# Stick-breaking attention: the scan's carry read in place, its copy and the constant column on GpSimd, v's high part on ScalarE

## The chip, the cores and the metric

The kernel runs on one core of one Trainium2 chip. A core has five engines that run side by side, each with its own in-order queue: TensorE (PE in the profile, with its weight loads as PEld), VectorE (DVE), ScalarE (ACT), GpSimd (POOL) and SyncE (SP), which here only issues DMAs. They share the on-chip memory SBUF (128 partitions) and, GpSimd excepted in this kernel, the accumulators' memory PSUM. The metric is the device time of one execution in microseconds (us); lower is better.

## The reference

One transformer block over 2048 tokens of width 1024, in float32. A projection gives two groups of heads. Four heads are differential attention (two softmax maps a head). Eight heads are stick-breaking attention, which is what the change touches:

```
z = q k^T * scale
mask = k_pos < q_pos
log_1mb = where(mask, log_sigmoid(-z), 0)
rem = cumsum from the right(log_1mb) - log_1mb
a = where(mask, exp(log_sigmoid(z) + rem), 0)
y = a @ v
```

So the weight of key s for query t is beta(t, s) = sigmoid(z) times the product of (1 - beta(t, j)) over all keys j between s and t. Then come the output projection, and a SwiGLU feed-forward of width 2816, each added to the residual trunk.

## The kernel before

Numbers are carried as a high and a low float16 part, so each product is three float16 matmuls. The heads are worked in eight groups: 0 to 3 are the differential heads, 4 to 7 hold two stick-breaking heads each. A generator `proj_stream` projects x for the groups tile by tile (128 tokens), and runs ahead of the attention, so that the projection of group g + 1 is interleaved with the attention of group g. Groups 4 to 6 are projected "turned" (`proj_turned`, q and k come out transposed), and every second tile `turned_out` (L345) takes q, k and v out of PSUM: ScalarE and VectorE write q's parts (L349, L350), and `split_psum` (L357) writes the high and low parts of k and of v. The high part goes to ScalarE (L360) or VectorE (L362), whichever `pick` finds to have the smaller sum of noted costs so far; the low part, which subtracts the high one, is always VectorE (L363). `pick` keeps these sums (`load`) for ScalarE, VectorE and GpSimd; `level` sets them to zero at every fourth row tile of the attention.

Stick-breaking attention (`sb_attn`, L595) goes over 16 row tiles i of 128 queries, over blocks b of up to 1024 keys from the right to the left, and over the two heads m. That is 48 blocks a group. One block is `stage_a` (L602):

- Two tiles of 1028 columns are taken, `be` and `om`, from one ring of nine buffers (`z4`, L263) which holds the block's products and its running products.
- Column n of `om`, right of the last key, gets the value with which the running product begins: the constant 8192 (a VectorE memset, L607) in a row's first block, else a copy of column 0 of the same head's block to the right (a VectorE tensor_copy, L609). Row tiles 8 to 15 have two blocks a head, so of a group's 48 blocks 32 set the constant and 16 copy.
- For each chunk of up to 512 keys, from the right: PE computes the scores into one of four PSUM buffers `sc` (L506, and L508 for the mask); ScalarE writes 1 - beta to `om` (L618) and beta to `sc` or to `be` (L619); VectorE runs the product scan from right to left in place in `om`, which begins with the column right of the chunk (L621); and beta times the running product one column to the right goes to `be` (L622).
- The product L622 is on GpSimd when the block has a second chunk and the group is 4 to 6 (`aside`), else on VectorE. It reads column n of `om` in the chunk that ends at n.
- `split_t` (L449) casts `be` to float16 on ScalarE (L89), makes the low part on GpSimd (L98), and has SP issue a transposing DMA to `aT` (L460).

`stage_b` then multiplies `aT` with v on PE (L517), five to seven blocks later. Every fourth row tile (in group 7 every second) `finish` normalizes the result.

The order on each engine is not the order of the program text. The tile framework collects all instructions with their dependences, and a planner lays them out by a simulated time line (`TileContext(nc, schedule_with_timeline_sim=True)`), with priorities given by the `pri` decorators: `stage_a` stands 200 places ahead (`PRI["at"]`). The framework also puts in the semaphore waits between engines and within one, and the waits for the release of a buffer. So each changed instruction is planned anew along with what is around it.

Of the kernel before, what the change touches and what calls it, by code (L numbers as in the profile page):

```python
# [16 lines left out]
ALU = mybir.AluOpType  # L17
# [4 lines left out]
S, D, P = 2048, 1024, 128  # L22
# [37 lines left out]
def block(tc, a, out):  # L60
    nc = tc.nc
    PE, ACT, DVE, POOL, SP = nc.tensor, nc.scalar, nc.vector, nc.gpsimd, nc.sync
    top = ExitStack()
    with top:
# [35 lines left out]
        def pri(k):  # L100
            def deco(f):
                @functools.wraps(f)
                def g(*args):
                    with tc.high_priority(PRI[k]) if PRI[k] else nullcontext():
                        return f(*args)
                return g
            return deco

        def nm(s):
            uid[0] += 1  # L110
            return f"{s}{uid[0]}"

        def c1(n=1, name="c"):
            t = cp.tile([P, n], F32, name=nm(name))
            return t
# [10 lines left out]
        mhalf = c1(16, "mh")  # L126
        DVE.memset(mhalf[:], -0.5)

        half = c1(2, "half")
        DVE.memset(half[:], 0.0)  # L130
        for m in range(2):
            DVE.memset(half[64 * m : 64 * m + 64, m : m + 1], 2.0 ** -11)

# [122 lines left out]
        with ExitStack() as ph1:  # L256
# [6 lines left out]
            def z4():  # L263
                return zp.tile([P, 1028], F32, tag="z4", bufs=ZB, name=nm("z4"))
# [79 lines left out]
            @pri("po")  # L344
            def turned_out(pq, pv, qT, kT, v, j):  # L345
                two = slice(j - 1, j + 1)
                q2, k2 = (pq[:, 256 * c : 256 * c + 256].rearrange("p (t n) -> p t n", t=2) for c in range(2))
                for m in range(2):
                    ACT.mul(qT[:, m, two, :], q2, half[:, m : m + 1])  # L349
                    DVE.scalar_tensor_tensor(qT[:, 2 + m, two, :], q2, half[:, m : m + 1], qT[:, m, two, :], op0=ALU.mult, op1=ALU.subtract)  # L350
                note("A", 800)
                note("D", 800)
                split_psum(kT[:, 0, two, :], kT[:, 1, two, :], k2, 256)
                vv = v[:, two, :].rearrange("p t (h s e) -> p t h s e", h=2, s=2)
                split_psum(vv[:, :, :, 0, :], vv[:, :, :, 1, :], pv[:, :256].rearrange("p (t h e) -> p t h e", t=2, h=2), 256)

            def split_psum(hi, lo, src, n):  # L357
                sc = 2.0 ** -11
                if pick(A=0.84 * n + 60, D=1.05 * n + 70) == "A":
                    ACT.mul(hi, src, sc)  # L360
                else:
                    DVE.tensor_scalar(hi, src, sc, None, op0=ALU.mult)  # L362
                DVE.scalar_tensor_tensor(lo, src, sc, hi, op0=ALU.mult, op1=ALU.subtract)  # L363
                note("D", 1.05 * n + 70)
# [230 lines left out]
            def sb_attn(g, G):  # L595
                last = {}
                front = []
                wide = [0]
                lag = PD + 2 if g < NG - 2 else PD

                @pri("at")
                def stage_a(i, m, b):  # L602
                    L = (i + 1) * 128
                    n = min(1024, L - 1024 * b)
                    be, om = z4(), z4()
                    if b == i // 8:
                        DVE.memset(om[:, n : n + 1], 8192.0)  # L607
                    else:
                        DVE.tensor_copy(om[:, n : n + 1], last[m][:, 0:1])  # L609
                    last[m] = om  # L610
                    for c in range((n - 1) // 512, -1, -1):
                        lo, hi = 512 * c, min(512 * c + 512, n)
                        w = hi - lo
                        sc = ps.tile([P, 512], F32, tag="sc", bufs=4, name=nm("sc"))
                        front.append(score_chunk(G, sc, i, 2 * b + c, m, w // P, b == i // 8 and hi == n, turned(g)))
                        aside = c == 1 and turned(g)
                        beta = be[:, lo:hi] if aside else sc[:, :w]
                        ACT.activation(om[:, lo:hi], sc[:, :w], AF.Sigmoid, scale=G["nkz"][:])  # L618
                        ACT.activation(beta, sc[:, :w], AF.Sigmoid, scale=G["kz"][:])  # L619
                        ov = om[:, lo:hi][:, ::-1]  # L620
                        DVE.tensor_tensor_scan(ov, ov, sc[:, :w], om[:, hi : hi + 1], op0=ALU.mult, op1=ALU.bypass)  # L621
                        (POOL if aside else DVE).tensor_tensor(be[:, lo:hi], beta, om[:, lo + 1 : hi + 1], ALU.mult)  # L622
                        note("A", 1.7 * w + 400)
                        note("D", 2.1 * w + 150)
                        note("P" if aside else "D", (1.65 if aside else 1.05) * w + 100)
                    wide[0] += 1
                    return n, split_t(be[:, :n], n, "A", "P", wide[0] if g < NG - 2 else None)

                ypd = {}

                def stage_b(i, m, b, n, aT):
                    with tc.issue_after(front[-1]):
                        stage_c(i, m, b, n, aT)

# [12 lines left out]
                for i in range(NT):  # L647
                    if i % 4 == 0:
                        level()
                    for b in range(i // 8, -1, -1):  # L650
                        for m in range(2):
                            n, aT = stage_a(i, m, b)
                            pend.append((i, m, b, n, aT))
                            if len(pend) > lag:
                                stage_b(*pend.pop(0))
                            done += n // P + CS
                            yield done / (272 + 48 * CS), (i + 1 if b == 0 and m == 1 else i)
                for u in pend:
                    stage_b(*u)
# [638 lines left out]
```

## Time and profile before

| what | value |
|---|---|
| median of 3 runs | 2703.69 us (2701.29 to 2709.12) |
| the profiled execution's own time | 2702.93 us |
| its span, first to last instruction | 2701.0 us |
| groups 4 to 6 of the attention, by the first and last rows of L607 and of GpSimd's L622 | 604 to about 1097 us |
| group 7, with the output projection | about 1097 to 1355 us |
| busy share of the span | PE 93%, DVE 73%, ACT 50%, POOL 56% |

The profile is of one execution. Its page lists busy time by engine, slices of the span, and the costliest groups of instructions by source line; views of the trace give the same for a stretch of time, the waits (which instruction waited for which), and the instructions in order of time. A row of groups reads: line, engine, operation, tile written and tiles read, shape, count, then busy us and mean ns of one, then the engine's idle time just before them and what ended it. A line can be that of a helper: L98 is any tensor_tensor made by `tt`. One VectorE instruction can start shortly before the one ahead has ended, so busy time and start-to-start distance differ.

### The profile page before, as it was taken

The page shows a single profiled execution, that of the slowest core. Times are in us where ns is not written, and L with a number is a line of the kernel's source. Part 1 is how long each engine was busy: PE and PEld are TensorE (multiplying, and loading weights), DVE is VectorE, ACT ScalarE, POOL GpSimd, SP SyncE. Part 2 cuts the span into 40 slices and gives each one's busy share as a digit, 9 for nine tenths or more (in the row PEclk, how much of TensorE's full clock was granted, in tenths as well). Part 3 has the DMA queues.
Part 4 walks back from the last instruction along what each step waited for, and adds up shares of the span by engine and source line. Part 5 has one row for each costly group of instructions (what it writes and reads, how often), then busy time and mean ns, then how long its engine had stood idle before and what let it go on. Part 6 is the DMA issues. An engine that isn't in the chain of part 4 may idle for free. (4 is left out here: it accounts for less than half of the span.)

```text
span 2701.0 us, 50505 instructions
## 1 busy us (share of the span) xinstructions
PE 2508.6 (93%) x19628; PEld 1507.6 (56%) x19628; DVE 1959.8 (73%) x3712; ACT 1344.7 (50%) x2487; POOL 1517.8 (56%) x1097
## 2 busy tenths in 40 slices
PE   7998989899988989889999999999999999999999
PEld 4655656577776776567774444444444444444444
DVE  6898879899989889887866877778685543433434
ACT  4665656567978878765634534435352112111121
POOL 2578767768767767545665755665564332322323
PEclk9999999999999999999999999999999999999999
DMA  6778697768989989997996566565748744635532
GB/s 221 211 163 184 143 200 172 172 145 183 195 175 185 178 166 206 208 205 203 230 317 232 211 232 219 207 239 183 253 171 330 304 159 157 234 132 184 202 110 94
DMA packets 619584, 534.40 MB, mean 198 GB/s; under 512 B 480640, under 2 KB 548224, under 8 KB 609104
## 3 DMA queue, kind: packets, MB, share of 16 engines
q1 hardware_dynamic: 617520, 529.09, 70.1%
q8 instruction: 154, 2.52, 0.4%
q0 software_dynamic: 512, 1.36, 0.2%
q14 instruction: 86, 0.70, 0.1%
q10 hardware_dynamic: 1312, 0.72, 0.1%
HBM read 261.08 MB, written 147.32 MB: 151 GB/s over the span
## 5 line engine op out<-in xcount | busy, mean ns | idle before, releaser
L98 POOL TENSOR_TENSOR s<-z,s 128x1024 f16<-128x1024 f32 (+7 forms) x288 | 471.5, 1646 | 141.8 <-ACT s L89 118.2
L506 PE MATMUL sc<-kT,qT 128*128 128x512 f16 (+3 forms) x1520 | 382.7, 354 | 51.1 <-DVE z L622 18.6
L1104 PE MATMUL pd<-wd,act 128*128 128x512 f16 x1764 | 392.8, 380 | 5.3 <-DVE cu L1038 4.7
L621 DVE TENSOR_TENSOR_SCAN z<-z,sc 128x512 f32<-128x512 f32 (+3 forms) x320 | 352.8, 1112 | 56.5 <-ACT sc L619 34.6
L325 PE MATMUL pj<-w,xt 128*128 128x384 f16 x1920 | 354.6, 333 | 17.1 <-ACT raw L374 5.8
L1004 PEld LDWEIGHTS <-wu 128*128 128x128 f16 x1848 | 181.9, 98 | 224.6 <-issue 12.8
L1004 PEld LDWEIGHTS <-wg 128*128 128x128 f16 x1848 | 181.3, 98 | 222.9 <-issue 9.3
L517 PE MATMUL yp<-v,aT 128*128 128x64 f16 (+1 forms) x4896 | 271.2, 205 | 36.9 <-DMA aT<-s 35.7
L517 PEld LDWEIGHTS <-aT 128*128 128x128 f16 x4896 | 239.1, 100 | 114.4 <-DMA aT<-s 46.7
L98 POOL TENSOR_TENSOR act<-cg,act 128x512 f16<-128x512 f32 x109 | 150.7, 1393 | 259.4 <-ACT act L1063 259.4
L1104 PEld LDWEIGHTS <-act 128*128 128x128 f16 x1764 | 172.9, 98 | 213.5 <-issue 7.2
L325 PEld LDWEIGHTS <-xt 128*128 128x128 f16 x1920 | 187.8, 99 | 147.2 <-issue 23.4
L89 ACT CAST s<-z 128x128 f16<-128x128 f32 (+7 forms) x215 | 173.3, 810 | 135.9 <-DMA aT<-s 44.6
L98 POOL TENSOR_TENSOR stages<-stages 128x512 f32<-128x512 f32 x97 | 171.4, 1767 | 116.5 <-DVE wg L220 42.2
L618 ACT ACTIVATE z<-sc,c 128x512 f32<-128x512 f32 (+3 forms) x320 | 211.2, 665 | 24.4 <-PE sc L506 12.4
L98 POOL TENSOR_TENSOR hs<-hs,cu 128x512 f32<-128x512 f32 x102 | 133.6, 1317 | 159.3 <-DVE hs L1110 59.7
L506 PEld LDWEIGHTS <-qT 128*128 128x128 f16 x1520 | 128.8, 99 | 119.7 <-issue 23.9
L831 PE MATMUL po<-wo,mt 128*128 128x256 f16 x1536 | 182.4, 279 | 12.6 <-DVE xf L834 8.6
L1063 ACT CAST act<-cg 128x512 f16<-128x512 f32 x126 | 76.7, 616 | 231.1 <-DVE cg L1069 192.7
L1110 DVE SCALAR_TENSOR_TENSOR hs<-pd,c,hs 128x512 f32<-128x512 f32 x144 | 106.0, 747 | 115.0 <-PE pd L1104 105.3
L341 PE MATMUL pj<-xt,w 128*128 128x128 f16 x2304 | 177.4, 222 | 6.2 <-DVE v L363 5.2
L1004 PE MATMUL pm<-X,wu 128*128 128x512 f16 x792 | 179.8, 381 | 2.1 <-ACT cg L1049 1.7
(254 smaller groups left out, 4812.3 us busy)
## 6 DMA issues: line engine op xcount, KB each, us to landing
xt<-xs SPq DMA_DIRECT2D x112, 512.0 KB, 4.5
hs<-hd SPq DMA_DIRECT2D x72, 512.0 KB, 4.5
hd<-hs SPq DMA_DIRECT2D x56, 512.0 KB, 5.9
split<-wg SPq DMA_DIRECT2D x11, 1792.0 KB, 6.9
split<-wu SPq DMA_DIRECT2D x11, 1792.0 KB, 6.7
split<-wd SPq DMA_DIRECT2D x11, 1792.0 KB, 6.8
wg<-split SPq DMA_DIRECT2D x11, 1792.0 KB, 7.5
wd<-split SPq DMA_DIRECT2D x11, 1792.0 KB, 9.0
```

The lines of the kernel that those rows point to most:

```text
L89: ACT.copy(dst, src)
L98: (DVE if e == "D" else POOL).tensor_tensor(dst, a_, b_, op)
L325: PE.matmul(pj[:, :384], lhsT=xv[:, xi, kt, :], rhs=G["w"][:, wi, kt, :], start=n == 0, stop=n == 23)
L341: PE.matmul(o, lhsT=x_ if c == 2 else w_, rhs=w_ if c == 2 else x_, start=n == 0, stop=n == 23)
L506: last = PE.matmul(sc[:, : 128 * w].rearrange("p (t n) -> p t n", n=P), lhsT=G["q"][i // 4][:, a_, i % 4, :], rhs=G["k"][q][:, b_, 0:w, :] ...
L517: PE.matmul(yp[:, y0 : y0 + wd], lhsT=aT[:, a_, :], rhs=v[:, v_ : v_ + wd], start=start and j == 0 and q == 0, stop=stop and j == nb - 1 a ...
L618: ACT.activation(om[:, lo:hi], sc[:, :w], AF.Sigmoid, scale=G["nkz"][:])
L621: DVE.tensor_tensor_scan(ov, ov, sc[:, :w], om[:, hi : hi + 1], op0=ALU.mult, op1=ALU.bypass)
L831: PE.matmul(po[:, sl], lhsT=mt[:, kt, P * xi : P * xi + P], rhs=wos[2 * h + n][wi][:, kt, :], start=q == 0, stop=q == 23)
L1004: PE.matmul(ps_[:].rearrange("p (t n) -> p t n", n=P), lhsT=wv[:, wo, wi, 128 * kt : 128 * kt + 128], rhs=X[xo][:, :, xi, kt, :], start=st ...
L1104: PE.matmul(po[:], lhsT=act[:, ao, xi, 128 * j : 128 * j + 128], rhs=W["d"][:, wo, wi, :], start=start and u == 0 and q == 0, stop=u == nu ...
L1110: DVE.scalar_tensor_tensor(dst, po[:], kd[:], src, op0=ALU.mult, op1=ALU.add)
```

## The change

Three things are edited.

1. A constant column `full` of 8192 is made once. The scan of a block's first chunk reads its initial value from `full`, or from column 0 of the block to the right (`last[m]`); the scan of a next chunk reads column 0 of the chunk to the right, which is the same place as before. So no scan reads column n of `om` any more.
2. Column n of `om` is still written, for the product L622, but by GpSimd: a memset in 128 blocks, and a tensor_scalar (times 1, plus 0) in 64 blocks.
3. `split_psum` takes a list of engines for the high part, and v's high part in `turned_out` is always on ScalarE. k's high part there, and all that `proj_out` splits, still choose between the two.

```
-        half = c1(2, "half")
-        DVE.memset(half[:], 0.0)
+        half = c1(3, "half")
+        full = half[:, 2:3]
+        DVE.memset(half[:, 0:2], 0.0)
+        DVE.memset(full, 8192.0)
...
-                split_psum(vv[:, :, :, 0, :], vv[:, :, :, 1, :], pv[:, :256]..., 256)
+                split_psum(vv[:, :, :, 0, :], vv[:, :, :, 1, :], pv[:, :256]..., 256, "A")

-            def split_psum(hi, lo, src, n):
+            def split_psum(hi, lo, src, n, he="AD"):
                 sc = 2.0 ** -11
-                if pick(A=0.84 * n + 60, D=1.05 * n + 70) == "A":
+                cost = {"A": 0.84 * n + 60, "D": 1.05 * n + 70}
+                if pick(**{e: cost[e] for e in he}) == "A":
...
                     if b == i // 8:
-                        DVE.memset(om[:, n : n + 1], 8192.0)
+                        begin = full
+                        POOL.memset(om[:, n : n + 1], 8192.0)
                     else:
-                        DVE.tensor_copy(om[:, n : n + 1], last[m][:, 0:1])
+                        begin = last[m][:, 0:1]
+                        POOL.tensor_scalar(om[:, n : n + 1], begin, 1.0, 0.0, op0=ALU.mult, op1=ALU.add)
...
-                        DVE.tensor_tensor_scan(ov, ov, sc[:, :w], om[:, hi : hi + 1], op0=ALU.mult, op1=ALU.bypass)
+                        DVE.tensor_tensor_scan(ov, ov, sc[:, :w], begin, op0=ALU.mult, op1=ALU.bypass)
+                        begin = om[:, lo : lo + 1]
```

More of the change, by code (lines that the diff above doesn't have):

```diff
@@ L354, in turned_out @@
                 vv = v[:, two, :].rearrange("p t (h s e) -> p t h s e", h=2, s=2)
-                split_psum(vv[:, :, :, 0, :], vv[:, :, :, 1, :], pv[:, :256].rearrange("p (t h e) -> p t h e", t=2, h=2), 256)
-            def split_psum(hi, lo, src, n):
+                split_psum(vv[:, :, :, 0, :], vv[:, :, :, 1, :], pv[:, :256].rearrange("p (t h e) -> p t h e", t=2, h=2), 256, "A")
+            def split_psum(hi, lo, src, n, he="AD"):
                 sc = 2.0 ** -11
-                if pick(A=0.84 * n + 60, D=1.05 * n + 70) == "A":
+                cost = {"A": 0.84 * n + 60, "D": 1.05 * n + 70}
+                if pick(**{e: cost[e] for e in he}) == "A":
                     ACT.mul(hi, src, sc)
```

## The prediction

> **What bounds the kernel now.** First the page. PE is busy for most of the span, and the chain of waits that ended last stays on feed-forward lines (L1104, L1004): its shares add up to 45% of the span, so it never reaches the lines edited here. It can't price the change; the stage has to.
>
> ```profile
> PE 2508.6 (93%) x19628; PEld 1507.6 (56%) x19628; DVE 1959.8 (73%) x3712; ACT 1344.7 (50%) x2487; POOL 1517.8 (56%) x1097
> ...
> PE 32%; DVE 6%; DMA 4%; ACT 1%; POOL 1%; issue 1%; SPq 0%; DVEq 0%; POOLq 0%; ACTq 0%
> ```
>
> Next, busy time by stretches: groups 4 to 6, group 7, and the feed-forward. The columns are PE, PEld, DVE, ACT, POOL, granted clock, DMA share, GB/s.
>
> ```profile
> 604.00:1097.00 493.00, 441.58 (x6559) 349.55 (x6560) 446.65 (x785) 406.05 (x742) 359.22 (x268) 0.98 0.94 187
> 1097.00:1355.00 258.00, 228.66 (x2364) 177.91 (x2361) 203.41 (x352) 164.03 (x304) 144.61 (x101) 0.95 0.85 208
> ...
> 1500.00:2701.00 1201.00, 1170.88 (x5448) 535.62 (x5446) 711.11 (x987) 355.00 (x465) 534.87 (x374) 0.99 0.56 201
> ```
>
> In groups 4 to 6 DVE is busy 446.65 of 493 us (91%), PE 90%, ACT 82%, POOL 73%. No engine is full; DVE and PE share the bound. PE is idle 493 - 441.58 = 51.4 us there, and 258 - 228.66 = 29.3 us in group 7. After 1500 us PE is busy 97%, and I assume that what is saved before arrives at the end one for one. Then the waits of PE in the two stretches, longest in total first (us, times, longest):
>
> ```profile
> PE sc L506 <- DVE z L622: 13.4, 19, 1.6
> PE yp L517 <- DMA aT<-s: 12.1, 12, 2.1
> PE pj L341 <- DVE v L363: 5.2, 6, 2.3
> PE sc L506 <- DVE z L607: 4.5, 7, 1.0
> PE sc L506 <- DVE z L621: 4.4, 11, 0.9
> PE sc L506 <- DVE z L609: 4.0, 7, 1.6
> PE wsc L182 <- DVE v L363: 3.8, 2, 3.5
> PE wsc L182 <- DVE kT L363: 2.0, 1, 2.0
> ...
> PE po L831 <- DVE xf L834: 8.6, 6, 3.6
> PE sc L506 <- DVE z L622: 5.2, 6, 2.1
> PE pj L325 <- DVE st L363: 3.5, 3, 1.9
> ```
>
> The first eight rows are groups 4 to 6, the last three group 7. Of PE's 51.4 us idle, DVE ended 13.4 + 5.2 + 4.5 + 4.4 + 4.0 + 3.8 + 2.0 = 37.3 us, or 0.73; in group 7 at least 17.3 of 29.3, or 0.59. PE stands still because VectorE has not yet freed a score buffer or a projection buffer. Two of the rows name the very lines that leave VectorE, L607 and L609.
>
> **The change part by part: what VectorE loses.** Rows of groups, the first three for groups 4 to 6, then the two lines over the whole span:
>
> ```profile
> L362 DVE TENSOR_SCALAR v<-pj 128x256 f16<-128x256 f32 x15 | 6.1, 408 | 0.6 <-PE pj L341 0.5
> L609 DVE COPY z<-z 128x1 f32<-128x1 f32 x48 | 5.9, 143 | 0.0
> L607 DVE MEMSET z<- 128x1 f32 x98 | 5.4, 59 | 0.3 <-POOL s L98 0.3
> ...
> L609 DVE COPY z<-z 128x1 f32<-128x1 f32 x64 | 8.2, 143 | 0.0
> L607 DVE MEMSET z<- 128x1 f32 x128 | 7.2, 59 | 0.3 <-POOL s L98 0.3
> ```
>
> By busy time groups 4 to 6 lose 6.1 + 5.9 + 5.4 = 17.4 us, and group 7 (8.2 - 5.9) + (7.2 - 5.4) = 4.1 us; 21.5 us in all is the upper end. The time line of VectorE gives the lower end, since its instructions overlap (start, us):
>
> ```profile
> 872.29 0.69 DVE L622 TENSOR_TENSOR z<-sc,z 128x512 f32<-128x512 f32 x1
> 872.89 0.14 DVE L609 COPY z<-z 128x1 f32<-128x1 f32 x1
> 872.96 1.27 DVE L621 TENSOR_TENSOR_SCAN z<-z,sc 128x512 f32<-128x512 f32 x1
> 872.99 0.06 DVE L607 MEMSET z<- 128x1 f32 x1
> 874.16 0.40 DVE L362 TENSOR_SCALAR v<-pj 128x256 f16<-128x256 f32 x1
> 874.47 0.47 DVE L350 SCALAR_TENSOR_TENSOR qT<-pj,half,qT 128x256 f16<-128x256 f32 x1
> ...
> 890.28 0.69 DVE L622 TENSOR_TENSOR z<-sc,z 128x512 f32<-128x512 f32 x1
> 890.90 1.27 DVE L621 TENSOR_TENSOR_SCAN z<-z,sc 128x512 f32<-128x512 f32 x1
> ...
> 1251.50 1.27 DVE L621 TENSOR_TENSOR_SCAN z<-z,sc 128x512 f32<-128x512 f32 x1
> 1252.69 0.45 DVE L834 SCALAR_TENSOR_TENSOR xf<-po,c,xf 128x256 f32<-128x256 f32 x1
> ```
>
> From product to scan it is 0.67 us with a copy between (872.29 to 872.96) and 0.62 without (890.28 to 890.90): a copy costs 0.05 us of the engine. From a scan to the next instruction it is 1.20 us with a memset between (872.96 to 874.16) and 1.19 without (1251.50 to 1252.69): next to nothing. v's high part costs 0.31 (874.16 to 874.47). So the lower end is 48 x 0.05 + 15 x 0.31 = 7.1 us in groups 4 to 6, and 16 x 0.05 = 0.8 us in group 7. I take the middle, 12.3 and 2.5 us, because neither end has the wait of a scan for its own engine's memset or copy, which also goes. PE's share of it is taken from the waits above: 12.3 x 0.73 = 9.0 us and 2.5 x 0.59 = 1.5 us, together 10.5 us.
>
> The Trainium skill prices a VectorE instruction on SBUF at 58 cycles plus one per element (VectorE: DVE Perf Modes, section on the TRN2 errata), which is an estimated 61 ns for one column. By that the 192 instructions would be 11.8 us where the rows have 15.4; the memset's row agrees with it (59 ns), the copy's is over twice as long (143 ns).
>
> **What the other engines gain.** ScalarE: nine of 24 were there already, 15 move.
>
> ```profile
> L360 ACT ACTIVATE v<-pj 128x256 f16<-128x256 f32 x9 | 4.0, 442 | 1.6 <-PE pj L341 1.6
> L360 ACT ACTIVATE kT<-pj 128x256 f16<-128x256 f32 x4 | 1.5, 385 | 0.6 <-DVE qT L350 0.6
> ```
>
> 15 x 0.442 = 6.6 us on an engine that is busy 82%. Behind each stand the sigmoids of the next chunk, for which the scan waits. The list of PE's waits names no ScalarE row in groups 4 to 6, so the least is 0; all of it on the path is 6.6; I take 1.0, the share 0.15. The low part L363 now always waits for ScalarE, and it frees the projection buffer. Since the forced choice adds to ScalarE's noted sum, up to four of k's high parts may come back to VectorE: at most 4 x 0.41 = 1.6 us of engine, taken as 0.3.
>
> GpSimd: the nearest rows are the memsets of one column at the kernel's start and the tensor_scalar of four columns.
>
> ```profile
> L1284 POOL MEMSET const-float32-1.0<- 128x1 f32 x1 | 0.1, 99 | 0.0
> L484 POOL TENSOR_SCALAR yrs<-yrs 128x4 f32<-128x4 f32 x16 | 5.9, 371 | 2.6 <-DVE yrs L483 2.4
> ```
>
> 128 x 0.10 + 64 x 0.37 = 36 us, of which groups 4 to 6 have 96 x 0.10 + 48 x 0.37 = 27 us: busy goes from 73% to 78%. What stands behind them in GpSimd's queue is the products it makes (L622, 96 of them) and the low parts (L98), then SP's transposing DMA, then PE's L517. That chain's wait is the 12.1 us row; grown by 27/359 it is 0.9 us more. The DMAs themselves stay as they are, in number and in queue.
>
> **The waits that are added.** The product L622 reads column n of `om`. Where GpSimd makes the product (n over 512, 32 blocks a group in groups 4 to 6), the writer is now on its own engine. Where VectorE makes it, it now waits for GpSimd: 16 blocks in each of groups 4 to 6 and all 48 of group 7, 96 in all, 80 of them on a memset that needs only a free buffer. What VectorE waits for GpSimd today is shown by two lines, for group 7:
>
> ```profile
> DVE z L228 <- POOL xrs L156: 3.3, 5, 1.1
> DVE y L486 <- POOL yrs L156: 2.2, 2, 1.3
> ...
> L228 DVE SCALAR_TENSOR_TENSOR z<-xf,xrs,bias 128x1024 f32<-128x1024 f32 x9 | 16.7, 1853 | 3.5 <-POOL xrs L156 3.3
> ```
>
> 3.3 us over nine is 0.37 us each, for a result that GpSimd can begin only when VectorE has just finished its input. The new writes are ready two sigmoids and a scan earlier, at least 1.27 us by the scan alone. The bounds are 0 and 96 x 0.37 = 36 us; I take 0.4 us in all, near 0, because GpSimd is idle 44% of group 7 and the writes have that lead. The buffer of `last[m]` is held until the next block's scan has read it instead of an earlier copy. The memset L607, which needs a free buffer of the same ring, sat idle 0.3 us over 98 times (its row above), so the ring is not short and I take 0; were it short, the most is one product (0.69 us) for each of 64 copies, 44 us.
>
> **Sum.** -10.5 + 1.0 + 0.3 + 0.9 + 0.4 = -7.9 us. The one edit that this leaves out is the scan's own wait, in the two rows of PE's waits behind L607 and L609 (4.5 + 4.0 us): of these I add 1 us as not yet in the engine's time. The planner lays the neighbours out anew too, which no row shows; I take 0, and bound it by two of PE's longest single waits above, 3.6 us each, for better or worse. -8.9 us against the profiled execution's 2702.9 gives 2694. The median of the runs, 2703.7, is 0.8 us above that execution, so the step is -0.36%. About 0.3%, or 8.1 us, is what a measurement of this kernel can tell from no change.
>
> **The rivals.** (1) VectorE alone is the bound, and everything freed arrives: -21.5 us, or 2681. For it speak the 91% and the 0.73; against it PE's own 90%. The Trainium skill's rule for the most contended engine (Perfetto Trace Analysis, Identifying the Most-Contended Engine) would have it so: it judges VectorE by occupancy and TensorE by weight loads, not by matmuls. Here weight loads are 349.55 of 493 us, 71%, so by that rule VectorE is the tightest.
>
> (2) Nothing measurable: VectorE's time goes back into waits for ScalarE. Its idle time in groups 4 to 6 is 493 - 446.65 = 46.4 us, and the sigmoids already end half of it:
>
> ```profile
> DVE z L621 <- ACT z L619: 11.2, 9, 4.0
> DVE z L621 <- ACT sc L619: 10.8, 16, 2.7
> ```
>
> By the lower ends the gain is 7.1 x 0.73 + 0.8 x 0.59 = 5.7 us; less the costs of 2.6 us above, and as much again for ScalarE being late, 0.5 us is left: 2702. Against it: the two rows of PE's waits behind L607 and L609.
>
> (3) Slower: GpSimd's column comes late. It is in order, and a memset that the planner puts behind a low part L98 waits until ScalarE's cast is done. VectorE's product then stands, and everything behind it, the score buffer among them. At 0.19 us a product, halfway between nothing and L228's 0.37, 96 products lose 18 us, and the time is 2702.9 - 8.9 + 18 = 2712. At 0.09 us a product it eats the gain, and from 0.18 us on the kernel is slower by over 0.3%. For it speak that group 7 has such a wait in every block; against it the lead of the write.
>
> **How the numbers follow.** The forecast has 0.40, of which 0.07 lies within 0.3%; rival 1 has 0.15, rival 2 0.20, rival 3 0.25. Faster by over 0.3% is 0.33 + 0.15 = 0.48; within 0.3% 0.07 + 0.20 = 0.27; slower 0.25. The likeliest's own range is 2687 to 2701, those 7 us either way. The range reaches below rival 1 by the wait of the scans, to 2676, and above rival 3 to 2720, with about one in ten outside on either side.
>
> **What would show it.** Right: no L607 or L609 on DVE, 128 and 64 on POOL; DVE busy in groups 4 to 6 down by about 17 us; the PE waits behind L607 and L609 gone and those behind L622 not grown; a wait DVE L622 behind POOL under 3 us; group 7 ending some 9 us earlier than 1355. Wrong: a row DVE L622 behind POOL L607 or L609 of over 10 us (rival 3); DVE's waits for ACT L619 grown from today's by as much as DVE lost (rival 2); L618 waiting for a buffer; or L363 waiting for L360 and PE's L341 behind it, which would mean that v's high part on ScalarE holds the projection buffer.

## The result and the profile after

The changed kernel takes 2734.72 us (median of 5 runs, 2731.25 to 2739.43) beside 2701.95 us of the kernel before (5 runs, 2700.21 to 2709.12). The ratio is 1.0116, with a 95% interval of 1.0103 to 1.0129: slower by about 31 us. The prediction was 2694 us with a range of 2676 to 2720, so it missed in sign, and the range did not hold the time.

In the changed kernel's line numbers the constant column is L611, its copy L614, the scan L626, the product L628, the sigmoids L623 and L624, v's high and low part L363, L365 and L366, the projections L327 and L343, the scores L509 and L511. The page of the changed kernel, its span and its busy time:

```profile
span 2734.4 us, 50628 instructions
...
PE 2509.9 (92%) x19628; PEld 1509.0 (55%) x19628; DVE 1941.6 (71%) x3506; ACT 1349.8 (49%) x2502; POOL 1530.6 (56%) x1289
```

Every engine does what was foretold: VectorE has 206 instructions and 18 us less, GpSimd 192 more, ScalarE 15 more, and PE is busy for the same 2510 us. Only the span grew, by 33.4 us. Groups 4 to 6, group 7 and the feed-forward, as stretches of the changed kernel (us, then PE, PEld, DVE, ACT, POOL busy, granted clock, DMA share, GB/s):

```profile
604.00:1112.00 508.00, 439.69 (x6533) 349.66 (x6532) 428.15 (x612) 410.60 (x755) 366.64 (x413) 0.96 0.88 178
1112.00:1386.00 274.00, 238.34 (x2441) 184.16 (x2437) 206.80 (x324) 167.82 (x308) 153.61 (x151) 0.95 0.82 205
1530.00:2734.00 1204.00, 1167.19 (x5442) 533.78 (x5439) 709.93 (x980) 354.49 (x464) 533.33 (x373) 1.00 0.56 201
```

VectorE is busy 428.15 us in groups 4 to 6, 18.5 less than before, while the stretch is 15 us longer; group 7 is 16 us longer. In the feed-forward PE is busy 1167.19 us, 1170.88 before, so what is lost ahead of it arrives at the end. The waits of VectorE in the two stretches of the changed kernel (us in total, times, longest):

```profile
DVE z L626 <- ACT sc L624: 57.8, 40, 5.4
DVE z L626 <- ACT z L624: 18.7, 10, 5.7
...
DVE z L628 <- POOL z L611: 4.8, 4, 1.8
DVE v L366 <- ACT v L363: 4.8, 2, 3.7
```

The same view of the kernel before, for its two stretches:

```profile
DVE z L621 <- ACT sc L619: 34.6, 29, 4.3
...
DVE z L621 <- ACT z L619: 11.2, 9, 4.0
...
DVE v L363 <- ACT v L360: 4.2, 3, 2.9
```

The scan waits for the sigmoids 76.5 us instead of 45.8: 30.7 us more, which looks like the whole loss. Whether it is cause or consequence the row can't say. PE's waits in the changed kernel:

```profile
PE sc L509 <- DVE z L628: 23.9, 30, 3.3
PE yp L520 <- DMA aT<-s: 22.7, 19, 3.9
PE pj L343 <- DVE v L366: 11.4, 8, 3.3
PE sc L509 <- DVE z L626: 8.3, 12, 2.5
PE wsc L184 <- DVE v L366: 8.2, 2, 4.7
```

and before, for the two stretches together (the prediction showed them apart):

```profile
PE sc L506 <- DVE z L622: 18.6, 25, 2.1
PE yp L517 <- DMA aT<-s: 13.2, 13, 2.1
...
PE sc L506 <- DVE z L607: 6.0, 8, 1.5
PE pj L341 <- DVE v L363: 5.2, 6, 2.3
PE sc L506 <- DVE z L609: 5.1, 8, 1.6
PE sc L506 <- DVE z L621: 4.4, 11, 0.9
PE wsc L182 <- DVE v L363: 3.8, 2, 3.5
```

The waits behind the memset and the copy are gone as foretold, but each of the five of the changed kernel is longer than it was. Where the time is lost can be read from the 320 scans, which both kernels make in the same order but for two pairs of neighbours (23 and 24, 169 and 170): the start of a scan less the start of the same scan before. Each row of such a table is one execution, and single scans move by a few us.

| scan | 0 | 100 | 104 | 212 | 228 | 240 | 260 | 316 | end of span |
|---|---|---|---|---|---|---|---|---|---|
| start before, us | 605.8 | 807.6 | 816.6 | 1037.4 | 1068.9 | 1095.1 | 1146.2 | 1346.6 | 2701.0 |
| the change, later by | 1.4 | 3.5 | 10.5 | 9.3 | 10.2 | 26.3 | 31.7 | 28.8 | 33.4 |

It is lost in places: around scan 104, and 21 us from scan 228 to 260, where group 6 gives way to group 7. Of the 7 us at scan 104 about 3 stay (in the median, scans 80 to 103 are 2.9 us late and scans 105 to 125 6.2). A change that is the same in all 192 blocks should not lose its time so. ScalarE's time line of the changed kernel shows what happens there (start, us, then what it waited for):

```profile
1077.16 1.00 ACT L89 CAST s<-z 128x896 f16<-128x896 f32 x1
1083.45 1.06 ACT L191 ACTIVATE wo<-z 128x1024 bf16<-128x1024 f32 x1 [5.29 <-DMA z<-in_w_out_dram]
...
1086.39 0.67 ACT L623 ACTIVATE z<-sc,c 128x512 f32<-128x512 f32 x1
...
1120.79 0.37 ACT L623 ACTIVATE z<-sc,c 128x128 f32<-128x128 f32 x1 [6.02 <-PE sc L511]
```

The same two places in the kernel before:

```profile
1065.15 1.12 ACT L189 ACTIVATE wo<-z 128x1024 bf16<-128x1024 f32 x1
...
1091.16 0.37 ACT L618 ACTIVATE z<-sc,c 128x128 f32<-128x128 f32 x1 [1.36 <-DVE wo L220]
```

L191 squares a row of the output weights, to find their scale. Neither it nor its load was touched. But in the changed kernel ScalarE stands 5.29 us because that load has not landed, with the sigmoids of the next scan queued behind. Then it stands 6.02 us for the first scores of group 7, where before it stood 1.36 us, and for VectorE. These look like matters of the order on the engines, which the planner made anew.

TensorE's granted clock is no rival for the large step: from 1060 to 1130 us it is 0.97, before 0.96. It is lowest from 1000 to 1060 us, 0.89 where it was 0.99 before, and there nothing is lost (10.5 us late at scan 104, 9.3 at scan 212). From 800 to 820 us, at the small step, it is 0.93 where it was 1.00; 0.07 of 20 us is an estimated 1.4 us at most.

### The profile page after: what moved, and what is told of

The parts are those of the page before. It is cut to its first block, busy times and chain, and to the rows that moved or that the text cites. A ratio compares the mean times of both kernels' runs of the same rounds, so it can differ in the third digit from the quotient of the medians.

```text
span 2734.4 us, 50628 instructions
## 1 busy us (share of the span) xinstructions
PE 2509.9 (92%) x19628; PEld 1509.0 (55%) x19628; DVE 1941.6 (71%) x3506; ACT 1349.8 (49%) x2502; POOL 1530.6 (56%) x1289
## 3 DMA queue, kind: packets, MB, share of 16 engines
q0 software_dynamic: 512, 1.36, 0.2%
## 5 line engine op out<-in xcount | busy, mean ns | idle before, releaser
L509 PE MATMUL sc<-kT,qT 128*128 128x512 f16 (+3 forms) x1520 | 385.4, 358 | 51.3 <-DVE z L628 23.9
L1110 PE MATMUL pd<-wd,act 128*128 128x512 f16 x1764 | 393.8, 380 | 10.2 <-DVE cu L1044 7.1
L327 PE MATMUL pj<-w,xt 128*128 128x384 f16 x1920 | 358.8, 335 | 17.1 <-ACT raw L377 5.8
L327 PEld LDWEIGHTS <-xt 128*128 128x128 f16 x1920 | 189.2, 100 | 149.4 <-issue 24.6
L623 ACT ACTIVATE z<-sc,c 128x512 f32<-128x512 f32 (+3 forms) x320 | 217.7, 680 | 37.6 <-PE sc L511 22.7
L837 PE MATMUL po<-wo,mt 128*128 128x256 f16 x1536 | 183.8, 280 | 17.9 <-DVE xf L840 8.4
L509 PEld LDWEIGHTS <-qT 128*128 128x128 f16 x1520 | 130.3, 100 | 119.1 <-DVE z L628 29.1
L343 PE MATMUL pj<-xt,w 128*128 128x128 f16 x2304 | 178.2, 225 | 13.6 <-DVE v L366 11.4
L1010 PE MATMUL pm<-X,wg 128*128 128x512 f16 x792 | 179.1, 379 | 0.0
```

The source lines that it names most:

```text
L327: PE.matmul(pj[:, :384], lhsT=xv[:, xi, kt, :], rhs=G["w"][:, wi, kt, :], start=n == 0, stop=n == 23)
L343: PE.matmul(o, lhsT=x_ if c == 2 else w_, rhs=w_ if c == 2 else x_, start=n == 0, stop=n == 23)
L509: last = PE.matmul(sc[:, : 128 * w].rearrange("p (t n) -> p t n", n=P), lhsT=G["q"][i // 4][:, a_, i % 4, :], rhs=G["k"][q][:, b_, 0:w, :] ...
L837: PE.matmul(po[:, sl], lhsT=mt[:, kt, P * xi : P * xi + P], rhs=wos[2 * h + n][wi][:, kt, :], start=q == 0, stop=q == 23)
L1010: PE.matmul(ps_[:].rearrange("p (t n) -> p t n", n=P), lhsT=wv[:, wo, wi, 128 * kt : 128 * kt + 128], rhs=X[xo][:, :, xi, kt, :], start=st ...
L1110: PE.matmul(po[:], lhsT=act[:, ao, xi, 128 * j : 128 * j + 128], rhs=W["d"][:, wo, wi, :], start=start and u == 0 and q == 0, stop=u == nu ...
```

## The experiments

Each run is compared with runs of the kernel before on the same chip; ratios carry 95% intervals.

**Each edit by itself, planned freely.** The first four kernels hold one or two of the edits and leave the order to the planner.

```
 e1_v_only:      before, and  split_psum(..., 256)  ->  split_psum(..., 256, "A")  for v
 e2_carry_only:  before, and  tensor_tensor_scan(ov, ov, sc, om[:, hi : hi + 1], ...)  ->  (..., begin, ...)
 e3_column_only: before, and  DVE.memset / DVE.tensor_copy  ->  POOL.memset / POOL.tensor_scalar
 e4_without_v:   the change, and  split_psum(..., 256, "A")  ->  split_psum(..., 256)
```

> The kernel before with v's high part in groups 4 to 6 always on ScalarE, and nothing else. Theory V (v's high part on ScalarE holds the projection buffer: in the changed kernel PE waited 13.5 us for projection buffers that VectorE's low part of v frees, 5.2 us before): 10 to 20 us slower than before, with that wait grown. Theory C (the column on GpSimd or the scan's carry is the cause): within 5 us of before. Theory N (every edit makes another plan, and a plan costs what it costs): any sign, and the parts do not add up to 33 us.

> The kernel before with the scan's initial value read in place (from the constant column or from the block to the right), while VectorE still writes column n for the product. Theory V: within 5 us of before. Theory B (the block to the right is held in the ring of nine buffers until the next block's scan): 10 to 30 us slower. The prediction's own steps would give up to 2 us faster, since only the scan's own wait goes.

> The kernel before with column n written by GpSimd, while the scan still begins from column n, as it did. Theory C (GpSimd's column is late): here the scan waits for GpSimd too, in 192 blocks, so 20 to 60 us slower, with the wait of the scan for GpSimd in the trace. Theory V: within 5 us of before or a little faster.

> The changed kernel with v's high part put back to the free choice: the carry in place and the column on GpSimd alone. Theory V: 0 to 10 us faster than before, as the prediction's sum says without v. Theory B or C: as slow as the changed kernel, 25 to 35 us slower than before. Theory N: anything between, and not the changed kernel less the first run's difference.

| edit | us | ratio |
|---|---|---|
| v's high part on ScalarE alone | 2740.29 | 1.0130 (1.0102 to 1.0159) |
| carry in place alone | 2714.05 | 1.0042 (1.0027 to 1.0057) |
| column on GpSimd alone | 2718.34 | 1.0055 (1.0036 to 1.0074) |
| carry and column, v free | 2720.29 | 1.0062 (1.0037 to 1.0087) |

Each edit alone is slower, the one for v as much as the whole change, and they do not add up: 35 + 11 + 15 us (the ratios less 1, times 2702) against 31 together. Since the planner made another order for each kernel, these runs mix the edit with its order. The next ones separate them.

**The same work in a given order.** In these kernels the program is laid out twice. The first time only serves to read the order in which the planner puts the instructions; the second time every instruction gets a dependence, without a semaphore, on the one before it on its engine in that order. The choices of `pick` are replayed too. The edits from here on are shown without the switches by which one file holds several variants.

```
+            for n in order:
+                i = traced[n]
+                p = ahead.get(i.engine)
+                if p is not None:
+                    tc.add_manual_dep(i, p, mybir.DependencyInfo(mybir.DependencyClass.NoSync, mybir.DependencyReason.DATA), reason="order")
+                ahead[i.engine] = i.name
```

An instruction that changes its engine stands in the new queue where its place in the common order puts it. Two constants say which work is done and whose order it takes:

```
 x1_change_old_order:        plan = before      work = all three edits
 x3_v_old_order:             plan = before      work = v's high part on ScalarE
 x4_carry_column_old_order:  plan = before      work = carry in place, column on GpSimd
 x2_old_work_new_order:      plan = the change  work = v's high part on ScalarE; column and carry as before
 x9_order_alone:             plan = the change  work = as before, v where the kernel before puts it
```

> All three edits, but each engine's instructions in the order that the planner gave the kernel before: the order is laid out first for the kernel before, and the changed program is then held to it, a moved instruction standing in its new engine's queue at the place it had in the common order. The engine choices of pick are those of the kernel before too, but for v. Theory N (the new order costs the time, the edits do not): 0 to 12 us faster than before, as the prediction's sum says. Theory W (the moved work itself costs it: GpSimd's column is late, v's high part holds the projection buffer): 15 us or more slower than before.

> v's high part on ScalarE alone, in the order of the kernel before. The free plan of the same edit was 38 us slower. Theory N: within 6 us of before. Theory V: 10 to 40 us slower, with PE's waits for projection buffers behind VectorE's low part of v grown from 5.2 us to over 10.

> The carry in place and the column on GpSimd, in the order of the kernel before, v left free. The free plan of the same edits was 17 us slower. Theory N: 0 to 10 us faster than before. Theory C: slower, with VectorE's product waiting for GpSimd by 5 us or more.

> The reverse: each engine in the order of the changed kernel, with its choices of pick (so v's high part stays on ScalarE), but column n written by VectorE and the scan beginning from it, as before. Theory N: about as slow as the changed kernel or slower, 30 to 45 us over before. Theory C: the column and the carry are what costs, so most of the 33 us comes back, within 15 us of before.

> The kernel before in all its work, engine for engine (column and the scan's begin on VectorE, v's high part where the kernel before puts it, 9 on ScalarE and 15 on VectorE), but every engine's instructions stand in the order that the planner made for the changed kernel. Theory N, the order itself is the cost: most of the changed kernel's loss comes without any of its edits, 2720 to 2732 us (1.007 to 1.011). Rival V, v's high part on ScalarE is most of it and the order only adds to it: in the old order v cost 1.0041, so what is left for the order alone is about 2735 - 11 - 7 = 2717 us or less (1.002 to 1.005). Rival S, the order harms only together with the moved work, which was what it was made for: within 0.2% of the kernel before, 2702 us.

| work | order | us | ratio |
|---|---|---|---|
| all three edits | before's | 2723.90 | 1.0078 (1.0050 to 1.0107) |
| v's high part on ScalarE | before's | 2715.72 | 1.0041 (1.0026 to 1.0056) |
| carry and column | before's | 2707.95 | 1.0016 (1.0003 to 1.0030) |
| v's high part on ScalarE | the change's | 2735.07 | 1.0108 (1.0080 to 1.0136) |
| none of the edits | the change's | 2739.97 | 1.0135 (1.0113 to 1.0158) |

The last row shows what the order does by itself. The kernel before, engine for engine the same work, is 36 us slower when its instructions stand in the order that the planner made for the changed kernel. With the edits that order takes 1.0116, without them 1.0135; the two can't be told apart. So the order is enough for the whole loss.

The first row shows what the edits do by themselves. All three in the old order are 21 us slower (13.5 to 29 by the interval), where I had expected 0 to 12 us faster. With the edits in, the old order would have saved only about 10 of the 31 us (1.0116 less 1.0078; 2 to 19 by the two intervals). So 36 and 21 us do not add up to the 31 of the change; either alone is enough for most of it.

Where the time is lost tells the two apart. The scans of these runs, later than before by (us):

| scan | 0 | 100 | 104 | 212 | 228 | 240 | 260 | 316 | end of span |
|---|---|---|---|---|---|---|---|---|---|
| all edits, before's order | -0.8 | 3.1 | 3.1 | 12.5 | 11.5 | 12.4 | 14.1 | 18.5 | 20.1 |
| no edits, the change's order | -1.7 | 1.6 | 8.1 | 10.5 | 11.8 | 26.6 | 29.8 | 31.6 | 34.1 |

In the old order the edits lose little by little, as a change in all blocks should, and 2.6 us from scan 228 to 260. The order alone loses 18.0 us there, like the changed kernel with its 21. So the loss of the changed kernel, as its trace shows it, is the order's. Why the edits' 21 us do not come on top of it stays open.

The stretches of the run of the order alone, none of whose work is changed:

```profile
604.00:1112.00 508.00, 436.51 (x6489) 347.36 (x6487) 434.15 (x758) 404.01 (x735) 351.63 (x266) 0.96 0.88 176
1112.00:1386.00 274.00, 237.19 (x2431) 184.08 (x2429) 208.68 (x368) 165.98 (x307) 147.89 (x103) 0.96 0.81 204
```

and two groups of its waits, of the scan for the sigmoids (L637 and L635 here) and of PE (the projection L351, the low part L374):

```profile
DVE z L637 <- ACT sc L635: 57.8, 42, 5.1
...
DVE z L637 <- ACT z L635: 16.0, 7, 5.7
...
PE pj L351 <- DVE v L374: 14.9, 8, 3.9
```

In the same stretches of the changed kernel PE is busy 3.2 and 1.2 us longer, ScalarE 6.6 and 1.8. The scan's waits are 73.8 us and the projection's 14.9, with nothing moved between the engines: the order alone makes both rows. It takes neither the freed VectorE time coming back nor v's high part holding the projection buffer, as one would read them from the two profiles alone.

In the old order the edits do have costs of their own, and there these readings hold in part. For v, the waits in the run of that edit alone (VectorE, then PE; the low part is L374, the high part L371):

```profile
DVE z L637 <- ACT sc L635: 38.0, 28, 4.3
DVE v L374 <- ACT v L371: 24.9, 13, 5.9
DVE z L637 <- ACT z L635: 16.4, 9, 5.6
```

```profile
PE pj L351 <- DVE v L374: 12.1, 9, 3.0
```

The low part waits 24.9 us for the high part, where it was 4.2. Ten of these waits, 17.8 us, are in groups 4 to 6, where there was none; in each of the ten ScalarE comes to the high part straight from other work (sigmoids, casts, squares), so the high part stood in its queue. PE waits 12.1 us for the projection buffer, where it was 5.2. The run is 11 us slower. For carry and column, groups 4 to 6 and group 7 of that run, and two views of its waits (the product is L639, GpSimd's column L619 and L623):

```profile
604.00:1095.00 491.00, 439.86 (x6541) 346.61 (x6539) 438.82 (x629) 403.74 (x739) 371.89 (x413) 0.99 0.94 185
1095.00:1363.00 268.00, 231.46 (x2395) 179.54 (x2394) 201.57 (x308) 165.21 (x305) 149.50 (x149) 0.95 0.86 203
```

```profile
DVE z L637 <- ACT sc L635: 41.5, 30, 4.3
DVE z L637 <- ACT z L635: 13.7, 10, 5.7
...
DVE z L639 <- POOL z L619: 5.6, 6, 1.4
...
DVE z L639 <- POOL z L623: 4.3, 3, 2.1
```

```profile
PE sc L517 <- DVE z L639: 30.0, 42, 2.8
...
PE sc L517 <- DVE z L637: 6.8, 16, 0.9
```

VectorE is busy 640.4 us (438.82 + 201.57) instead of 650.1: 9.7 us less. Its waits for the sigmoids are 55.2 us instead of 45.8: 9.4 us more. In groups 4 to 6 alone VectorE is busy 7.8 us less, its waits for the sigmoids are 5.1 us more (27.1 from 22.0), and 5.6 us of waits for GpSimd's memset are new. So the freed time turned into waiting, in part for ScalarE and in part for GpSimd, and PE's waits behind the memset and the copy came back behind the product: 30.0 + 6.8 = 36.8 us, where before it was 18.6 + 6.0 + 5.1 + 4.4 = 34.1 behind L622, L607, L609 and L621. Along the scans of this run the change is nil through groups 4 to 6 (2.2 us early at scan 0, 1.6 early at scan 240), and 8 us are lost in group 7 (6.5 late at scan 316), where I had expected 0 to 10 us faster in all. The product's waits for GpSimd's memset, 5.6 us, lie in groups 4 to 6, where the time stood still; those for GpSimd's copy, 4.3 us, in group 7.

**Is VectorE the bound at all?** One run adds to VectorE what the change takes away: every column is written twice, in the old order. Another leaves all high parts of v on VectorE.

```
 x5_column_twice:
+                    if b == i // 8: DVE.memset(om[:, n : n + 1], 8192.0)
+                    else:           DVE.tensor_copy(om[:, n : n + 1], last[m][:, 0:1])
 x6_v_on_vector:
-                split_psum(..., 256)
+                split_psum(..., 256, "D")
```

> The kernel before, in its own order, with each of the 192 column writes on VectorE done twice (a second memset or copy of the same column right behind the first): 15.4 us more busy time of VectorE, 3 to 15 us of engine time. The prediction's conversion (0.73 of what VectorE is freed of or loaded with reaches PE): 5 to 11 us slower. Theory L (VectorE is paced by a loop with ScalarE and PE, and small instructions stand in its idle time): within 3 us of before, as the fixed-order run of the reverse edit showed no gain in groups 4 to 6.

> The kernel before, in its own order, with v's high part always on VectorE: the nine that were on ScalarE move, the mirror image of the run that moved 15 the other way and was 11 us slower. Theory V (what costs is that VectorE's low part waits for a high part queued behind ScalarE's sigmoids): 2 to 7 us faster, with VectorE's wait for ScalarE's v gone in groups 4 to 6. The prediction's conversion: 9 x 0.41 x 0.73 = 2.7 us slower.

Written twice, the column costs 14.0 us: 2714.87 us, 1.0052 (1.0034 to 1.0070). The stretches of that run, summed:

```profile
sum 767.00, PE 671.85 PEld 524.91 DVE 666.51 ACT 571.26 POOL 505.94; mean PE 335.92 PEld 262.45 DVE 333.25 ACT 285.63 POOL 252.97
```

VectorE is busy 666.51 us, 16.5 more than the 650.06 before (446.65 + 203.41): added load costs 14.0 / 16.5 = 0.85 us a us (0.56 to 1.15 by the interval). The 9.7 us taken away gave nothing, but there the writes went to GpSimd, for which VectorE then waited; no run takes work off VectorE without giving it to another engine. With all of v's high parts on VectorE it is 2706.61 us, 1.0022 (1.0009 to 1.0034): slower, where I had expected 2 to 7 us faster. So v is dearer on either engine alone than where `pick` puts it.

**The best of the parts.** Carry in place, the column on GpSimd in groups 4 to 6 only, v's high part on VectorE, in the old order.

```
 x7_best_of_parts:
+                        (POOL if turned(g) else DVE).memset(om[:, n : n + 1], 8192.0)
+                        begin = om[:, lo : lo + 1]
+                split_psum(..., 256, "D")
```

> In the order of the kernel before: the carry in place, the column on GpSimd in groups 4 to 6 alone and on VectorE in group 7 (where the fixed-order run lost 8 us), and v's high part on VectorE. Theories L and V: 2 to 9 us faster than before. The prediction's steps: about 5 us faster too, but then by VectorE's freed time.

2702.88 us, 1.0008 (0.9996 to 1.0020): no change, where 2 to 9 us faster was expected. With the column of group 7 back on VectorE, the 8 us that the run of carry and column lost there are not lost (1.1 us early at scan 240, 1.4 early at scan 316). No version here beat the kernel before.

**Where in the order.** The first run puts the two first squares of the output weights (L191) eleven instructions further back in ScalarE's queue, in the changed kernel's own order. The other two take half of the new order each, for the old work: the new order up to the 216th scan and then the old one, and the reverse.

```
 x8_wout_later:     plan = the change, work = all three edits
+                order.insert(act[10], order.pop(k))      # the first two squares of w_out
 x10_new_then_old, x11_old_then_new:   work = as before
+    cut = sorted(seat[n] for n in scans)[215]
+    order = first[:cut] + [n for n in then if n not in head]
```

> The changed kernel in its own order, except that the two squares of the first output weights (ScalarE, 1083 to 1087 us, behind which ScalarE stood 5.3 us for their load) stand eleven places later in ScalarE's queue. If that stall makes the jump of 10 to 20 us at the end of group 6: 8 to 20 us faster than the changed kernel, so 12 to 25 us slower than before. If the jump only shows there and the order is at fault as a whole: within 4 us of the changed kernel, 28 to 36 us slower than before.

> The kernel before in all its work, its instructions in the changed kernel's order up to the 216th of the 320 scans (near the end of group 6) and in the old order from there. If the loss lies where it shows, +8 us at scan 216 and the rest behind it, this run is 8 us slower than before and stays there: about 2711 us (1.003). Rival: what the new order does early makes it pay late (work put off, which the old order would then have to catch up), so that the loss comes here too: 2725 us or more.

> The other half: the old order up to the 216th scan, the changed kernel's order from there. If the loss lies where it shows, between scans 216 and 260 at the boundary of group 6 and group 7, it comes whole in this run: about 24 us, 2726 us (1.009), with ScalarE's 5 us wait for w_out and its 6 us wait for group 7's first scores. Rival: the late part of the new order is only slow because of what stands late when it begins; then this run is within 0.3% of before.

| run | us | ratio |
|---|---|---|
| squares later | 2726.61 | 1.0099 (1.0077 to 1.0122) |
| new order, then old | 2717.98 | 1.0068 (1.0046 to 1.0091) |
| old order, then new | 2720.68 | 1.0086 (1.0060 to 1.0112) |

The scans of these runs, later than before by (us); the run with the whole new order is in the table above. The run that begins in the old order, with the old work, is 7.0 us early at scan 0 already, so a loss is read along a row:

| scan | 0 | 100 | 104 | 212 | 228 | 240 | 260 | 316 | end of span |
|---|---|---|---|---|---|---|---|---|---|
| new, then old | -8.3 | -5.0 | 1.4 | 3.9 | 12.4 | 12.4 | 12.9 | 12.7 | 15.4 |
| old, then new | -7.0 | -6.3 | -6.3 | -6.0 | -6.9 | 9.3 | 12.5 | 9.9 | 15.9 |
| the change, squares later | -4.4 | -2.3 | 4.6 | 3.6 | 4.4 | 17.9 | 22.8 | 19.5 | 21.9 |

Both halves of the order lose on their own. Up to scan 212 the new order loses 12.2 us with the old one to follow (-8.3 to 3.9) and 12.2 us with the new one to follow (-1.7 to 10.5). From scan 228 to 260 it loses 19.4 us after a stretch in the old order (-6.9 to 12.5) and 18.0 us after its own. So the late loss does not follow from work that was put off. The first half's run cost more than I expected, 18 us instead of 8: I had read 8 us off the absolute column without taking off the start of scan 0, and 8.5 us more go at the seam between the orders (3.9 to 12.4). The second half's run costs 23 us by its ratio, near the 24 expected. It has both of ScalarE's stalls, here in its time line (L199 is the square, L634 the sigmoid):

```profile
1065.42 1.06 ACT L199 ACTIVATE wo<-z 128x1024 bf16<-128x1024 f32 x1 [4.63 <-DMA z<-in_w_out_dram]
...
1103.84 0.37 ACT L634 ACTIVATE z<-sc,c 128x128 f32<-128x128 f32 x1 [5.99 <-PE sc L519]
```

The wait for the load is that of a load issued too late for where the square stands. In the changed kernel SP issues it at 1076.85 us, and ScalarE comes to the square when its cast ends, 1077.16 + 1.00 = 1078.16, 1.3 us later:

```profile
1076.85 1.75 SPq L808 DMA_DIRECT2D z<-in_w_out_dram  x2
```

In the kernel before, SP issues it 5.7 us ahead of the square, which began at 1065.15:

```profile
1059.47 1.14 SPq L802 DMA_DIRECT2D z<-in_w_out_dram  x2
```

During the second stall, PE works through a block of the projection that stands ahead of the first scores of group 7, and these then wait for group 7's transposed keys to land. In the changed kernel, PE and SP:

```profile
1111.99 5.20 PE L327 MATMUL pj<-w,xt 128*128 128x384 f16 x31
...
1117.99 0.49 PE L509 MATMUL sc<-kT,qT 128*128 128x128 f16 x4 [0.37 <-DMA kT<-st]
```

```profile
1114.82 1.34 SPq L412 DMA_TRANSPOSE kT<-st  x1
```

and in the kernel before:

```profile
1086.52 0.22 PE L506 MATMUL sc<-kT,qT 128*128 128x128 f16 x1 [0.39 <-DVE z L621]
```

```profile
1077.75 1.33 SPq L409 DMA_TRANSPOSE kT<-st  x1
```

So group 7's keys are late: SP issues their transposing DMA 37 us later than before, 3.2 us ahead of the first scores, where it was 8.8. They are late because their projection is: its fourth tile, which completes the first keys, ends on PE at 1104 us, 1071 before. The scans show what it costs. From the last one of group 6 to the first of group 7 it is 13.3 us in the changed kernel, 12.7 with the order alone and 14.2 with its second half, but 1.2 before and with all edits in the old order. These 12 us of the 21 go with the place at which the new order puts the projection of group 7. That is read from the traces; no run moves this projection by itself.

With the squares set back the wait for the load is gone, but the cast ahead of the square now waits 3.28 us for VectorE's product, and between scan 228 and 240 the run still loses 13.5 us where the change loses 16.1. By these scans that stall is worth about 3 us and not the 5.3 it lasts; the ratios (1.0099 and 1.0116) can't be told apart. What was argued from the stall's length was too much.

At scan 104 PE stands 4.65 us at L184 for VectorE's low part of v, 4.58 with the order alone, where before it stood 0.27. The rest of the loss of this order stays open. The carry in place alone, in the old order, was not tried.

## Why the prediction was wrong

Two steps failed. The first is "The planner lays the neighbours out anew too, which no row shows; I take 0", bounded by two waits of 3.6 us, so by 7.2 us either way. The new order alone costs 36 us, five times that bound, and the changed kernel loses its time in the same places. The bound was drawn from waits that the old order has, and so could say nothing of the waits that another order would bring.

The second is the sum of the edits' own terms, -8.9 us. Held to the old order, the three edits are 21 us slower, so the forecast would have had the wrong sign without a new order too. Its step of -0.36% also counts 0.8 us that only lie between the profiled execution and the median; -8.9 us is -0.33%. The terms, one by one:

- **VectorE's freed time, -10.5 us.** It did not arrive. In the old order, with the column gone from VectorE and the carry in place, groups 4 to 6 took the same time. PE's waits behind VectorE, which gave the shares 0.73 and 0.59, say who releases PE last. They do not say that PE is released earlier when VectorE has less to do, since VectorE in turn waits for the sigmoids, and here for GpSimd. The rule for the most contended engine (the Trainium skill, Perfetto Trace Analysis, Identifying the Most-Contended Engine), which stood behind rival 1's 2681 us, is borne out half way here: loading VectorE costs 0.85 us a us, while 9.7 us moved from it to GpSimd gave nothing.
- **v's high part, +1.0 us.** The mechanism that the prediction named as its own refutation (the low part waits for ScalarE, PE's projection behind it) exists in the old order and costs 11 us there, more than the upper bound of 6.6. The bound counted only ScalarE's added time and not the wait in its queue, 17.8 us on VectorE in groups 4 to 6.
- **GpSimd's column, +0.4 us.** The waits of the product are 9.9 us in the old order and 4.8 us for the memset in the change's order, in few places (nine and four). Rival 3's mechanism is there, but smaller than its 18 us: in the old order the column on GpSimd goes with 8 us in group 7, and with none in groups 4 to 6. GpSimd's instructions were cheaper than taken, by the changed kernel's groups:

```profile
L614 POOL TENSOR_SCALAR z<-z 128x1 f32<-128x1 f32 x64 | 13.8, 221 | 13.6 <-DVE z L626 13.5
...
L611 POOL MEMSET z<- 128x1 f32 x128 | 11.6, 99 | 2.8 <-DVE z L628 2.7
```

  25.4 us instead of 36. L611, which needs a free buffer of the ring, was idle for 2.8 us over 128: the ring, taken as 0, stayed out of it. But L614 stands 13.5 us for the scan whose column it copies, with GpSimd's products and low parts behind it.
- **The chain to aT, +0.9 us.** In the old order that row of PE's waits did not grow (13.3 us, from 13.2). In the change's order it is 22.7 with the edits and 13.6 without them, at about the same time of the kernel, so the time does not hang on it.
- **The scan's own wait, -1.0 us.** The two rows of PE's waits did go, and came back behind the product (36.8 us from 34.1).
- **k's high parts, +0.3 us.** None came back: in both traces 20 of the 24 are on VectorE and four on ScalarE.

Rival 2, VectorE's time goes into waits for ScalarE, is in part what carry and column do in the old order: those waits grew by 9.4 us for 9.7 freed, beside 9.9 us of new waits for GpSimd. It gives no loss of 31 us, and the order alone makes the changed kernel's row of such waits. No rival had the order as its mechanism.

## What to carry to other kernels

Where a planner lays out the instructions, an edit has two prices, that of the work and that of the new order, and the second can be the larger; hold the order fixed to tell them apart before a row of waits is believed. In a stage in which several engines share the bound, load added to one of them cost most of its time here, while load moved from it to another engine gave nothing: before freed time is counted as time, read what that engine will wait for next. When a step between two groups grows, look first at when the next group's inputs are issued. When a split value's two halves are made on two in-order queues, count the wait in the other queue, not the instruction that moves.

## What the hardware showed that was not expected

Writing a column of one element a partition on VectorE costs the kernel more time than VectorE's start-to-start distances let expect: 192 added writes cost 14.0 us, 0.073 us each (0.05 to 0.10 by the interval), where the time line had shown 0.05 us for a copy and nearly nothing for a memset. The Trainium skill's 58 cycles and one per element (VectorE: DVE Perf Modes, on the TRN2 errata), an estimated 61 ns, lies within that interval. On GpSimd a tensor_scalar of one column took 221 ns in the mean, where the four-column one had taken 371.

TensorE's granted clock goes with the order of the instructions. From 800 to 820 us it is 0.83 to 0.93 in the changed kernel and in the four runs that have its order there, and 1.00 in the kernel before and in the seven runs that have the old order there. Which follows from which the traces do not say.
